# Two-layer decoder trunk on one core: the MLP's second product with one more seven-product tile per pass, its sums gathered by accumulating DMAs

## The chip, the core and the metric

One core of a Trainium2 chip runs the whole kernel in one launch. The metric is device time in microseconds (us), the median of several executions. Before the change it is 2025.09 us (three runs, 2024.75 to 2025.41).

## What is computed

A decoder trunk of two layers over 256 tokens with 2048 channels, in float32. Layer one is a gated short convolution and an MLP, layer two latent attention and an MLP; every half layer ends in a layer norm of the scaled input plus what the half layer gives. The change touches the two MLPs alone:

```python
D_MODEL = 2048; SEQ = 256; D_FF = 4 * D_MODEL; ALPHA = (2 * DEPTH) ** 0.25

def sq_relu_mlp(x, w1, w2):
    return jnp.square(jax.nn.relu(x @ w1)) @ w2

for layer in range(DEPTH):
    mix = short_conv_mixer(...) if layer < N_A else mla_mixer(...)
    h = layer_norm(ALPHA * h + mix, ln_g[layer, 0], ln_b[layer, 0])
    h = layer_norm(ALPHA * h + sq_relu_mlp(h, mlp_w1[layer], mlp_w2[layer]), ln_g[layer, 1], ln_b[layer, 1])
```

## The kernel before

*Precision.* Every float32 operand is split in a high and a low part of type float32r (`split`, L120): ScalarE casts the high part (L122), VectorE subtracts it (L123). A product is three matmuls, high by high, high by low and low by high. `dot` (L282) issues three matmuls of 512 columns. In `mm_run` (L206) the activation is the moving operand with its high and low part side by side: `high` (L200) has 512 columns, `low` (L204) 256.

*Weights.* All weights are one list, `stream`, in the order of use. `take` (L172) hands out the next items and prepares those that follow, until more than `LOOK` = 5 tiles are ahead. A plain item is one transfer of 128 x 1024 (512 KB) from the SP queue into one of five `raw` buffers, split into one of eight pairs of `hi` and `lo` buffers. An item of two transfers (`w2f`) is a tile for seven products: `prepare` (L143 to L166) forms from its four 128 x 512 blocks the combinations that the algorithm wants, with one VectorE operation of 1024 columns (L155) and two of 512 (L158, L161), and splits three tiles of 1024 columns and one of 512 (`t4`). It counts as three tiles.

*The MLP* (`mlp`, L567) goes over the 8192 hidden channels in eight steps q of 1024. A step has two parts. In the first, eight units of W1 (`products`, L273, 32 matmuls each) give 8 x 128 hidden channels into PSUM; `hidden` (L649) brings them out (`whole`, L337: a ScalarE copy and a VectorE add), applies the squared ReLU and splits the result. In the second these 1024 channels are multiplied with W2 and added to `acc` (128 partitions, two halves of 128 tokens, 2048 columns). `acc` has four blocks of 512 columns; `block(n, t)` is block n for the token half t.

*Seven products.* For q = 1 to 6 (`FAST`) the first two blocks go by the Strassen-Winograd scheme: the two token halves, two K tiles of 128 and two blocks make a 2 x 2 by 2 x 2 product, which takes seven products of blocks instead of eight (`FACTORS`, L325). The activation's side wants four combinations, `forms` (made by `form`, L639, in the memory with the tag "a2"). `first_pair` (L603) takes four such tiles, one for each pair of K tiles, and sums the seven products in seven PSUM banks (`KEPT`). `keep` (L595) then adds each bank on VectorE: products 2, 3 and 4 into `acc`, products 1, 5, 7 and 6 (`OWN`) into `sums`. Blocks 2 and 3 follow one after the other by plain products (`down`, L296: four items each, two token halves, two banks), and `put` (L585) adds them to `acc` on VectorE. In the second MLP two small pieces of the residual are turned by TensorE between them (`extra`). In q = 7 `fold` (L612) brings `sums` into `acc` once, six VectorE adds spread over the W1 units; q = 0 and q = 7 have no seven-product tiles.

*Banks.* PSUM has eight banks. The W1 units of q = 1 to 7 use banks 0 and 1 in turn. `first_pair` uses banks 2 to 7 and 0, `down` banks 1 and 2, then 3 and 4.

*Order.* Each engine runs its instructions in the order in which the program has them; the scheduler of the framework fixes that order, also across loops (the preparation of weights is moved ahead of the evacuations that stand before it in the code). TensorE's order is that of the code: per step 256 matmuls of W1, 84 of four seven-product tiles, 96 of eight plain tiles.

## Time and profile before

| | |
|---|---|
| median of three runs | 2025.09 us |
| the profiled execution | 2024.51 us |
| its span, first to last instruction | 2022.5 us |
| TensorE busy | 2015.9 us, 11240 matmuls |
| VectorE busy | 1605.8 us |
| ScalarE busy | 1176.4 us |
| GpSimd busy | 2.3 us, 21 instructions |
| moved by DMA | 385.83 MB, 191 GB/s on average |

A profile line of a group names the source line, the engine, the operation, what is written and read, the shapes and the count; behind the bar stand the busy time, the mean duration in ns, and the idle time of the engine ahead of these instructions with what ended it. PE is TensorE's matmul, PEld its load of weights, DVE VectorE, ACT ScalarE, POOL GpSimd, SP SyncE, which issues the loads. A line of the timeline has the start in us from the start of the span, the duration, and what idle time lay ahead. Matmuls overlap, so the distance of their starts counts, not their duration. A line of the stretches has the window, its length, and for each engine its busy time in it, then TensorE's granted clock, the busy share of the DMA engines, and GB/s.

### The profile page before, as it was taken

What the parts mean: (1) busy time and instruction counts of PE and PEld (TensorE: products, weight loads), DVE (VectorE), ACT (ScalarE), POOL (GpSimd) and SP (SyncE); (2) the same over time, 40 slices, a digit from 0 to 9 for tenths busy, and PEclk for the clock granted to TensorE, in tenths of its full rate; (3) what the DMA queues carried; (4) which work ended last, traced back from release to release, by engine and by line L of the source; (5) the groups of instructions that cost most, each with busy time, mean ns of one, the idle gap of its engine ahead of it and who ended that gap; (6) DMA issues with size and microseconds to landing.
All of it is one profiled execution on the core that took longest, in us unless ns stands there. A gap on an engine that the chain in (4) does not pass through costs nothing.

```text
span 2022.5 us, 30067 instructions
## 1 busy us (share of the span) xinstructions
PE 2015.9 (100%) x11240; PEld 1761.4 (87%) x11240; DVE 1605.8 (79%) x2472; ACT 1176.4 (58%) x1802; POOL 2.3 (0%) x21
## 2 busy tenths in 40 slices
PE   9999999999999999999999999999999999999998
PEld 8888888988888888888889998898888888888886
DVE  8667677788797987979688978776879798797966
ACT  6444445676565665656556655567656556565651
POOL 0000000000000000000000000000000000000000
PEclk9999999999999999999999999999999999999999
DMA  9666666564756647466654544656475664746663
GB/s 322 201 189 188 189 189 192 174 196 144 250 164 202 221 153 249 151 224 209 210 173 152 182 126 137 193 178 194 135 247 176 198 224 140 252 160 205 220 202 119
DMA packets 106849, 385.83 MB, mean 191 GB/s; under 512 B 11856, under 2 KB 12624, under 8 KB 106448
## 3 DMA queue, kind: packets, MB, share of 16 engines
q1 hardware_dynamic: 106560, 383.79, 59.5%
q8 instruction: 88, 1.44, 0.3%
q14 instruction: 57, 0.47, 0.1%
q10 hardware_dynamic: 144, 0.13, 0.0%
HBM read 381.78 MB, written 2.10 MB: 190 GB/s over the span
## 4 chain that ended last, share of the span: by engine, by line
PE 99%; DVE 0%; issue 0%; ACT 0%; DVEq 0%
PE ps_u L200 20%; PE ps_l L200 13%; PE ps_u L204 11%; PE ps_d L284 7%; PE ps_d L286 7%; PE ps_d L285 7%; PE ps_l L204 7%; PE ps_f L285 4%; PE ps_f L286 4%; PE ps_f L284 4%; PE ps_w L234 1%; PE ps_w L232 1%; PE ps_w L233 1%; PE ps_g L234 1%; PE ps_g L232 1%; PE ps_g L233 1%
## 5 line engine op out<-in xcount | busy, mean ns | idle before, releaser
L123 DVE TENSOR_TENSOR lo<-raw,hi 128x1024 fp32r<-128x1024 f32 x710 | 860.0, 1222 | 314.9 <-ACT hi L122 243.2
L122 ACT CAST hi<-raw 128x1024 fp32r<-128x1024 f32 x710 | 742.4, 1050 | 460.5 <-PE ps_u L200 107.9
L200 PE MATMUL ps_u<-xhl,hi 128*128 128x512 f32 x1792 | 621.0, 391 | 0.0
L204 PE MATMUL ps_u<-xhl,lo 128*128 128x256 f32 x1792 | 499.5, 280 | 0.0
L200 PEld LDWEIGHTS ps_u<-xhl,hi 128*128 128x128 f32 x1792 | 334.2, 187 | 72.4
L204 PEld LDWEIGHTS ps_u<-xhl,lo 128*128 128x128 f32 x1792 | 338.6, 189 | 1.8
L284 PE MATMUL ps_d<-hi,h 128*128 128x512 f32 x640 | 249.8, 390 | 0.0
L286 PE MATMUL ps_d<-hi,h 128*128 128x512 f32 x640 | 249.1, 389 | 0.0
L285 PE MATMUL ps_d<-lo,h 128*128 128x512 f32 x640 | 249.0, 389 | 0.0
L200 PE MATMUL ps_l<-xhl_a,hi 128*128 128x512 f32 x704 | 244.1, 393 | 0.0
L204 PE MATMUL ps_l<-xhl_a,lo 128*128 128x256 f32 x704 | 195.4, 279 | 0.0
L200 PEld LDWEIGHTS ps_l<-xhl_a,hi 128*128 128x128 f32 x704 | 132.1, 188 | 29.9
L286 PEld LDWEIGHTS ps_d<-hi,h 128*128 128x128 f32 x640 | 120.1, 188 | 25.0
L284 PEld LDWEIGHTS ps_d<-hi,h 128*128 128x128 f32 x640 | 120.1, 188 | 25.0 <-DVE fh L341 0.3
L285 PEld LDWEIGHTS ps_d<-lo,h 128*128 128x128 f32 x640 | 120.2, 188 | 24.7
L204 PEld LDWEIGHTS ps_l<-xhl_a,lo 128*128 128x128 f32 x704 | 131.9, 188 | 0.2
L654 ACT ACTIVATE fp<-fp 128x256 f32<-128x256 f32 x96 | 40.0, 416 | 73.7 <-DVE fp L341 72.9
L200 PE MATMUL ps_l<-z,hi 128*128 128x512 f32 x240 | 82.4, 391 | 0.0
L122 ACT CAST hi_t<-raw_t 128x1024 fp32r<-128x1024 f32 x48 | 50.4, 1050 | 42.2 <-DVE raw_t L155 33.4
L234 PE MATMUL ps_w<-xd,hi 128*128 128x258 f32 x256 | 72.8, 284 | 0.0
L232 PE MATMUL ps_w<-xd,hi 128*128 128x258 f32 x256 | 72.6, 284 | 0.0
L233 PE MATMUL ps_w<-xd,lo 128*128 128x258 f32 x256 | 72.4, 283 | 0.0
(261 smaller groups left out, 3132.3 us busy)
## 6 DMA issues: line engine op xcount, KB each, us to landing
raw<-in_w_dram SPq DMA_DIRECT2D x416, 512.0 KB, 4.4
raw<-in_w2f_dram SPq DMA_DIRECT2D x96, 512.0 KB, 3.6
raw<-in_w_in_dram SPq DMA_DIRECT2D x88, 512.0 KB, 4.3
raw<-in_w_out_dram SPq DMA_DIRECT2D x32, 512.0 KB, 3.7
raw<-in_w_o_dram SPq DMA_DIRECT2D x32, 512.0 KB, 4.2
raw<-in_w_kv_dram SPq DMA_DIRECT2D x10, 512.0 KB, 3.5
raw<-in_w_q_dram SPq DMA_DIRECT2D x8, 512.0 KB, 4.6
raw<-in_w_uk_dram SPq DMA_DIRECT2D x8, 512.0 KB, 4.6
```

What stands on the lines that cost most here:

```text
L122: nc.scalar.copy(hi, src)
L123: nc.vector.tensor_tensor(lo, src, hi.bitcast(F32), ALU.subtract)
L200: nc.tensor.matmul(ps, w[blk // 8][0][:, blk % 8, :], x, start=first, stop=False)
L204: nc.tensor.matmul(ps[:, :T], w[blk // 8][1][:, blk % 8, :], x[:, :T], start=False, stop=last)
L232: nc.tensor.matmul(ps[:, :W], hi, x[k][:, :W], start=k == 0, stop=False)
L233: nc.tensor.matmul(ps[:, :W], lo, x[k][:, :W], start=False, stop=False)
L234: nc.tensor.matmul(ps[:, :W], hi, x[k][:, W:], start=False, stop=k == NC - 1)
L284: nc.tensor.matmul(ps, x[0], w[0], start=first, stop=False)
L285: nc.tensor.matmul(ps, x[0], w[1], start=False, stop=False)
L286: nc.tensor.matmul(ps, x[1], w[0], start=False, stop=last)
L654: nc.scalar.activation(f, f, AF.Relu)
```

## The change

For q = 1 to 6 the second part has a new order, `down_pairs`, in place of `first_pair` and two calls of `down`:

- Blocks 2 and 3 come first, both at once, in four banks. Their four pairs of K tiles follow `MIXED`: the first by one seven-product tile, the other three by plain products. The plain products add to the banks of products 22, 3, 2 and 4 of that tile ("22" is the product of block 3 with the second token half); the tile's products 1, 5, 7 and 6 are done after it and go into `sums`, which is twice as large. One matmul of each step, the high by low one of product 22 in the last K tile, is issued as two of 256 columns (`EVEN`). `w2f` holds both pairs of blocks.
- Blocks 0 and 1 follow with four seven-product tiles in seven banks. Their sums are copied by ScalarE into `stage` (the memory of `forms`) and added to `acc` and `sums` by DMAs with `accum_op`, issued from the Pool queue. In q = 1 the `OWN` products are copied to `sums` directly.
- The W1 units use four banks in turn; which four, and which the second part uses, moves on by one with each step.
- `fold` has eight adds of 1024 elements per partition. Plain tiles of the second part are taken with a lookahead of 6 instead of 5.

```diff
--- before.py
+++ after.py
@@ -35,6 +35,8 @@
 NB = 4
 BW = D // NB
 FAST = range(1, NQ - 1)
+MIXED = "sppp"
+EVEN = (QC - 1, "22")
 FIRST = (0, 1, 2, 3, 4, 6, 8, 12, 16)
 LEAD = 4
 HEAD = 4
@@ -82,10 +84,13 @@
         out = []
         for q in range(NQ):
             out += halves(w1[l, q * QC:(q + 1) * QC])
-            plain = halves(w2[l, q, 2:] if q in FAST else w2[l, q])
-            fast = [(w2f[l, q, j, 0], w2f[l, q, j, 1]) for j in range(QC // 2)] if q in FAST else []
-            at = 0 if q or q not in FAST else len(plain) // 2
-            out += plain[:at] + fast + plain[at:]
+            if q not in FAST:
+                out += halves(w2[l, q])
+                continue
+            for j, kind in enumerate(MIXED):
+                out += [(w2f[l, q, 1, j, 0], w2f[l, q, 1, j, 1])] if kind == "s" else \
+                    halves(w2[l, q, 3, j]) + halves(w2[l, q, 2, j])
+            out += [(w2f[l, q, 0, j, 0], w2f[l, q, 0, j, 1]) for j in range(QC // 2)]
         return out
 
     stream += mlp_stream(0) + halves(w_kv) + halves(w_q)
@@ -169,14 +174,14 @@
 
         return 1 if len(stream[i]) == 1 else 3
 
-    def take(halves=2):
+    def take(halves=2, look=LOOK):
 
         i = state["next"]
         state["next"] += halves
         ahead = -sum(size(j) for j in range(i, i + halves))
         for j in range(i, len(stream)):
             ahead += size(j)
-            if ahead > LOOK:
+            if ahead > look:
                 break
             if j >= state["split"]:
                 prepare(j)
@@ -279,10 +284,11 @@
             yield ps
 
 
-    def dot(ps, w, x, first, last):
+    def dot(ps, w, x, first, last, two=False):
 
         nc.tensor.matmul(ps, x[0], w[0], start=first, stop=False)
-        nc.tensor.matmul(ps, x[0], w[1], start=False, stop=False)
+        for at in (slice(0, T), slice(T, 2 * T)) if two else (slice(None),):
+            nc.tensor.matmul(ps[:, at], x[0], w[1][:, at], start=False, stop=False)
         nc.tensor.matmul(ps, x[1], w[0], start=False, stop=last)
 
     def held(x, t):
@@ -319,20 +325,20 @@
                     dot(ps, wide_rows(ws[n, k // 2], k % 2), held(x[k], t), k == 0, k == len(x) - 1)
                 put(n, t, ps)
 
-    OWN, KEPT = ("1", "5", "7", "6"), (2, 3, 4, 5, 6, 7, 0)
+    OWN = ("1", "5", "7", "6")
 
 
     FACTORS = (("3", "S4", "22"), ("1", "11", "11"), ("5", "S1", "T1"), ("7", "S3", "T3"),
                ("2", "12", "21"), ("6", "S2", "T2"), ("4", "22", "T4"))
 
-    def fast_products(ps, x, forms, j, n):
+    def fast_products(ps, x, forms, j, fresh, ready):
 
         b, = take(1)
         a = {"11": held(x[2 * j], 0), "12": held(x[2 * j + 1], 0), "22": held(x[2 * j + 1], 1)}
         for i in range(4):
             a[f"S{i + 1}"] = [forms[:, j, o, i * P:(i + 1) * P] for o in range(2)]
         for p, l, r in FACTORS:
-            dot(ps[p], b[r], a[l], j == 0, j == n - 1)
+            dot(ps[p], b[r], a[l], p in fresh, p in ready)
 
     def whole(ps, out):
 
@@ -590,36 +596,70 @@
             else:
                 nc.vector.tensor_tensor(block(n, t), block(n, t), ps, ALU.add)
 
-        sums = fast.tile([P, 4, BW], F32, name=f"sums{idx}")
-
-        def keep(p, ps):
-
-            at = sums[:, OWN.index(p)] if p in OWN else block(*{"2": (0, 0), "3": (1, 0), "4": (0, 1)}[p])
-            if q == 0 or q == FAST[0] and p in OWN:
+        sums = fast.tile([P, 4, 2, BW], F32, name=f"sums{idx}")
+
+        def keep(p, g, ps, staged=None):
+
+            at = sums[:, OWN.index(p), g, :] if p in OWN else \
+                block(*{"2": (2 * g, 0), "3": (2 * g + 1, 0), "4": (2 * g, 1), "22": (2 * g + 1, 1)}[p])
+            if q == FAST[0] and p in OWN:
                 nc.scalar.copy(at, ps)
+            elif staged is not None:
+                nc.scalar.copy(staged, ps)
+                nc.gpsimd.dma_start(at, staged, accum_op=ALU.add)
             else:
                 nc.vector.tensor_tensor(at, at, ps, ALU.add)
 
-        def first_pair(h, forms, banks):
-
+        def down_pairs(h, forms, busy, free):
+
+            ps = {p: psum("ps_d", bank) for p, bank in zip(("22", "3", "2", "4"), free)}
+            fresh = {"22", "3", "2", "4"}
+            for j, kind in enumerate(MIXED):
+                if kind == "s":
+                    first, last = j == MIXED.index("s"), j == MIXED.rindex("s")
+                    if first:
+                        ps.update({p: psum(f"ps_f{p}", bank) for p, bank in zip(OWN, busy)})
+                        fresh.update(OWN)
+                    fast_products(ps, h, forms, j, fresh, OWN if last else ())
+                    fresh &= {"22"}
+                    if last:
+                        for p in OWN:
+                            keep(p, 1, ps[p])
+                    continue
+                if extra and q <= NB and j == len(MIXED) - 1:
+                    for t in range(2):
+                        extra(block, q - 1, t, busy[2 + t])
+                for nb, two in ((3, ((1, "22"), (0, "3"))), (2, ((0, "2"), (1, "4")))):
+                    w, = take(1, LOOK + 1)
+                    for t, p in two:
+                        for kk in range(2):
+                            k = 2 * j + kk
+                            dot(ps[p], wide_rows(w, kk), held(h[k], t), p in fresh, k == QC - 1, (k, p) == EVEN)
+                            fresh.discard(p)
+                    if j == len(MIXED) - 1:
+                        for _, p in two:
+                            keep(p, 1, ps[p])
             n = QC // 2
+            banks = (*busy, *free)
             ps = {p: psum(f"ps_f{p}", bank) for (p, _, _), bank in zip(FACTORS, banks)}
             for j in range(n):
-                fast_products(ps, h, forms, j, n)
-            for p in ps:
-                keep(p, ps[p])
+                fast_products(ps, h, forms, j, ps if j == 0 else (), ps if j == n - 1 else ())
+            stage = act.tile([P, 7, BW], F32, tag="a2", name=f"stage{idx}_{q}")
+            for i, p in enumerate(ps):
+                keep(p, 0, ps[p], stage[:, i, :])
+            return (banks[7], *banks[:3]), banks[3:7]
 
         def fold():
 
             s1, s5, s7, s6 = (sums[:, i] for i in range(4))
-            both = acc[:, 1, :2 * BW].rearrange("p (b c) -> p b c", b=2)
-            right = acc[:, :, BW:2 * BW]
-            two = lambda v: v.unsqueeze(1).to_broadcast([P, 2, BW])
-            for d, a, b in ((block(0, 0), block(0, 0), s1), (s6, s6, s1), (block(1, 0), block(1, 0), s6),
-                            (s7, s7, s6), (both, both, two(s7)), (right, right, two(s5))):
+            c = acc.rearrange("p t (g b c) -> p t b g c", g=2, b=2)
+            for d, a, b in ((c[:, 0, 0], c[:, 0, 0], s1), (s6, s6, s1), (c[:, 0, 1], c[:, 0, 1], s6), (s7, s7, s6),
+                            (c[:, 1, 0], c[:, 1, 0], s7), (c[:, 1, 1], c[:, 1, 1], s7),
+                            (c[:, 0, 1], c[:, 0, 1], s5), (c[:, 1, 1], c[:, 1, 1], s5)):
                 nc.vector.tensor_tensor(d, a, b, ALU.add)
                 yield
 
+        busy, free = (0, 1, 2, 3), (4, 5, 6, 7)
         for q in range(NQ):
             ht = act.tile([P, QC, 2 * T], F32R, tag="c", name=f"h{idx}_{q}")
             h = [ht[:, k, :] for k in range(QC)]
@@ -681,7 +721,7 @@
                 acc = act.tile([P, 2, D], F32, tag="a1", name=f"acc{idx}")
             else:
                 folds = fold()
-                for m, ps in enumerate(products(QC, xhl, TURNED, (0, 1))):
+                for m, ps in enumerate(products(QC, xhl, TURNED, busy)):
                     hidden(m, ps, whole)
                     if q == NQ - 1:
                         next(folds, None)
@@ -695,12 +735,7 @@
                 for n in range(NB):
                     down(h, put, n)
             else:
-                first_pair(h, forms, KEPT)
-                for n, banks in ((2, (1, 2)), (3, (3, 4))):
-                    down(h, put, n, banks)
-                    if extra and n == 2 and q <= NB:
-                        for t in range(2):
-                            extra(block, q - 1, t, 5 + t)
+                busy, free = down_pairs(h, forms, busy, free)
 
     def to_wide(block, put, h):
 
@@ -1093,7 +1128,8 @@
         "w_o": _units(a["mla_w_o"][0]),
         "w1": np.stack([_units(w) for w in a["mlp_w1"]]),
         "w2": np.stack([np.stack([_rows(q) for q in w.reshape(NQ, QC * P, D)]) for w in a["mlp_w2"]]),
-        "w2f": np.stack([np.stack([_pairs(q[:, :2 * BW]) for q in w.reshape(NQ, QC * P, D)]) for w in a["mlp_w2"]]),
+        "w2f": np.stack([np.stack([np.stack([_pairs(q[:, 2 * g * BW:2 * (g + 1) * BW]) for g in range(2)])
+                                   for q in w.reshape(NQ, QC * P, D)]) for w in a["mlp_w2"]]),
         "cosT": np.tile(cos, (4, 1)),
         "sinT": np.tile(np.concatenate([sin, -sin]), (2, 1)),
         "mask": np.concatenate([tri, np.zeros((P, P), np.float32), tri], axis=1),
```

## The prediction

> A *pass* below is one of the twelve turns of the loop over q that the change touches (q = 1 to 6 of each of the two MLPs). Its *W1 part* is eight units of 32 matmuls, its *down part* what the functions `first_pair` and `down` issue. A *seven-product tile* is one item of the weight stream with w2f weights, a *plain tile* one with w2 weights. A time with a + counts from the end of a pass's W1 part.
>
> **What bounds the kernel now.** I read the page first: shares of the engines, then the chain of waits.
>
> ```profile
> span 2022.5 us, 30067 instructions
> PE 2015.9 (100%) x11240; PEld 1761.4 (87%) x11240; DVE 1605.8 (79%) x2472; ACT 1176.4 (58%) x1802; POOL 2.3 (0%) x21
> PE 99%; DVE 0%; issue 0%; ACT 0%; DVEq 0%
> ```
>
> TensorE is busy all of the span and the chain that ended last is 99% TensorE: the time is the number of matmuls times the distance of their starts. That distance is not the mean duration in the groups, since matmuls overlap. The timeline of PE has it; its first column is the start.
>
> ```profile
> 583.26 0.39 PE L284 MATMUL ps_f<-hi,forms 128*128 128x512 f32 x1
> ...
> 602.34 0.39 PE L284 MATMUL ps_d<-hi,h 128*128 128x512 f32 x1
> ...
> 624.10 0.39 PE L200 MATMUL ps_u<-xhl,hi 128*128 128x512 f32 x1
> ```
>
> From 583.26 to 602.34 lie the 84 matmuls of four seven-product tiles, from there to 624.10 the 96 of eight plain tiles: 0.2271 and 0.2267 us each, with no room for a gap. The stretches of this pass, by engine:
>
> ```profile
> core 0: us, PE busy (x) PEld busy (x) DVE busy (x) ACT busy (x) POOL busy (x), PEclk, DMA share, GB/s
> 538.87:583.24 44.37, 44.37 (x257) 39.10 (x256) 34.96 (x52) 27.64 (x45) 0.00 (x0) 1.00 0.50 153
> 583.24:602.32 19.08, 19.08 (x86) 15.79 (x85) 17.62 (x24) 12.10 (x16) 0.00 (x0) 1.00 0.52 157
> 602.32:624.10 21.78, 21.78 (x97) 18.02 (x96) 19.15 (x21) 11.74 (x12) 0.00 (x0) 1.00 0.89 313
> 538.87:624.10 85.23, 85.23 (x437) 72.91 (x436) 71.73 (x96) 51.48 (x72) 0.00 (x0) 1.00 0.60 195
> 965.04:1009.40 44.36, 44.36 (x257) 39.09 (x256) 26.50 (x34) 25.92 (x44) 0.53 (x1) 1.00 0.69 211
> ```
>
> The rows are W1 part, seven-product tiles, plain tiles, the whole pass, and the W1 part of q = 7; the granted clock is 1.00 in each. VectorE is busy 71.73 of 85.23 us (13.5 free), but 17.62 of 19.08 while the seven-product tiles run; the DMA engines are 89% busy only while the plain tiles run. So a matmul that goes is worth its whole 0.227 us, as long as VectorE, ScalarE and the DMAs keep ahead.
>
> **The change, part by part.** *Matmuls.* The first K tile pair of blocks 3 and 4 goes from eight dots of three matmuls to seven: 12 x 3 x 0.2267 = 8.16 us go. `EVEN` splits one 512-wide matmul in two 256-wide. The trace has no such split; the nearest rows are 256-wide matmuls that follow one another:
>
> ```profile
> 1145.04 0.28 PE L218 MATMUL ps_q<-lat,lo 128*128 128x256 f32 x1
> ...
> 1146.95 0.28 PE L219 MATMUL ps_q<-lat,hi 128*128 128x256 f32 x1
> ```
>
> 16 distances in 1.91 us, 0.119 us each. Two cost 0.239 instead of 0.227: 12 x 0.012 = 0.14 us. From both sides: nothing, or two full loads of weights of 0.188 us (first row of the next fence) in place of 0.227, 12 x 0.15 = 1.8 us. I take 0.14, whose rows have the same width and each its own load.
>
> *VectorE and ScalarE.* One seven-product tile takes the place of two plain tiles. The costs are in the groups:
>
> ```profile
> L285 PEld LDWEIGHTS ps_d<-lo,h 128*128 128x128 f32 x640 | 120.2, 188 | 24.7
> L123 DVE TENSOR_TENSOR lo<-raw,hi 128x1024 fp32r<-128x1024 f32 x710 | 860.0, 1222 | 314.9 <-ACT hi L122 243.2 <-issue 46.7 <-PE ps_l L204 21.6
> L155 DVE TENSOR_TENSOR raw_t<-raw,raw 128x1024 f32<-128x1024 f32 x48 | 58.5, 1220 | 5.4 <-DMA raw<-in_w2f_dram 5.2
> L161 DVE TENSOR_TENSOR raw<-raw 128x512 f32<-128x512 f32 x48 | 33.1, 689 | 0.8
> L123 DVE TENSOR_TENSOR t<-raw,t 128x512 fp32r<-128x512 f32 x48 | 32.8, 684 | 0.0
> L601 DVE TENSOR_TENSOR sums<-sums,ps_f 128x512 f32<-128x512 f32 x40 | 26.4, 681 | 0.0
> L122 ACT CAST hi<-raw 128x1024 fp32r<-128x1024 f32 x710 | 742.4, 1050 | 460.5 <-PE ps_u L200 107.9 <-PE ps_d L286 106.3 <-PE ps_l L200 98.0
> L122 ACT CAST t<-raw 128x512 fp32r<-128x512 f32 x48 | 29.6, 616 | 2.1 <-DVE raw L161 2.0
> L599 ACT COPY sums<-ps_f 128x512 f32<-128x512 f32 x8 | 4.5, 586 | 0.2 <-PE ps_f L286 0.2
> ```
>
> VectorE, per pass: one split more (1.222), one `raw_t` (1.220) and three of half size (L158, L161 and the split of `t`, 0.686 each by the two rows shown), 4.50 us more; of eleven adds from PSUM (seven `keep`, four `put`) eight stay, 3 x 0.681 = 2.04 less. Net +2.46 of 13.5 us free: hidden on average. ScalarE, per pass: 1.050 + 0.616 for casts and seven copies of 0.586, +5.8 us on 51.48 of 85.23: hidden. The bytes from HBM stay (a seven-product tile is 1 MB, two plain tiles are 1 MB). `fold` has eight adds of 1024 elements instead of four of 512 and two of 1024: 6 x 1.222 - 4 x 0.681 = 4.6 us more in q = 7, where VectorE is busy 26.50 of 44.36 us: hidden.
>
> *Order.* Six plain tiles now stand between the first seven-product tile and the other four, and these four end the pass. Until the last dot of the last one (4.76 + 6 x 2.72 + 3 x 4.76 + 6 x 0.68 = +39.4 us) VectorE has: the rest of the last W1 unit (an evacuation, two half splits, four forms of 0.28, 2.9), eight adds from PSUM (5.4), about three of the six plain splits (3.7; the eight weight buffers let the others run in the W1 part), four seven-product tiles of 3 x 1.222 + 1.220 + 3 x 0.686 = 6.94 each (27.8): 39.8 us. But its operations overlap when nothing makes them wait:
>
> ```profile
> 559.39 1.22 DVE L155 TENSOR_TENSOR raw_t<-raw,raw 128x1024 f32<-128x1024 f32 x1 [0.51 <-DMA raw<-in_w2f_dram]
> 560.53 1.22 DVE L123 TENSOR_TENSOR lo<-raw,hi 128x1024 fp32r<-128x1024 f32 x1
> 561.67 0.28 DVE L644 TENSOR_TENSOR sf<-fp 128x128 f32<-128x128 f32 x1
> ```
>
> 1.14 us apart for a duration of 1.22; over 46 operations that is 3.7 us less, 36.1 against 39.4. I take it as hidden, since four such tiles keep VectorE 92% busy today (17.62 of 19.08) without a wait on TensorE. At 92% and no overlap it would be 39.8 / 0.92 = 43.3, 3.9 us late in each pass. Both ends stay for the range.
>
> *Banks.* The sixth dot of the first tile writes the PSUM bank of the last W1 unit, at +3.40 us (15 x 0.2267). The evacuation of that unit, in a pass whose W1 part ends at 1711.38:
>
> ```profile
> 1711.38 0.39 PE L284 MATMUL ps_f<-hi,forms 128*128 128x512 f32 x1
> ...
> 1714.42 0.42 DVE L341 TENSOR_TENSOR fp<-ps_u,t 128x256 f32<-128x256 f32 x1
> ```
>
> It ends at +3.46, a wait of 0.06 us. Before, that bank was first wanted after the 84 matmuls of the seven-product tiles. I take 0.1 us in all; if one more cast and split came ahead (1.05 + 1.22) it would be 2.3 us in each pass. With four W1 banks instead of two an evacuation may come three units late instead of one; no W1 part is longer than its 256 matmuls today, so nothing is gained.
>
> *Accumulating DMAs.* The last seven sums are copied by ScalarE into `stage` and added by 76 DMAs of 256 KB from the Pool queue, where 21 small instructions stand today. `stage` has the memory of `forms`: the copies wait for the last use of `forms`, the sixth dot of the last tile, and the next pass writes `forms` only after all seven DMAs have landed. In the program of the changed kernel that wait stands in ScalarE's order behind the evacuation of the second W1 unit, as here:
>
> ```profile
> 641.80 0.36 ACT L340 COPY t<-ps_u 128x256 f32<-128x256 f32 x1
> 642.08 0.62 ACT L122 CAST forms<-sf 128x512 fp32r<-128x512 f32 x1
> ```
>
> 642.08 - 624.10 = 18.0 us after the W1 part begins. No accumulating DMA is in the trace. Nearest rows, issue to landing:
>
> ```profile
> raw<-in_w_dram SPq DMA_DIRECT2D x416, 512.0 KB, 4.4
> out_dram<-acc SPq DMA_DIRECT2D x8, 256.0 KB, 2.4
> xres<-in_xT_dram SPq DMA_DIRECT2D x2, 256.0 KB, 6.9
> ```
>
> `out<-acc` moves 256 KB of the same tile: seven one after another take 16.8 us and land before 18.0. From both sides: all at once after the last copy, or 6.9 us each, 48 us. I take 2.4, as size and tile agree: no wait. The Trainium skill ("DMA: Bandwidth & Descriptors", section "Anatomy of one DMA — SWDGE (gpsimd) path") gives about 2.0 us plus bytes over 436 GB/s; an estimate from it is 2.6 us each, 18.2 in a row, and the sum would stay as it is, since ScalarE would wait 0.2 us. No run here shows it yet.
>
> *Sum.* -8.16 + 0.14 + 0.1 = -7.9 us. The profiled execution took 2024.51 us (span 2022.5 and 2.0 around it), 0.6 below the median 2025.09; so 2016.6 for such an execution, and 2017.2 as a median.
>
> **Rivals.**
>
> *The accumulations come late* (slower). ScalarE and VectorE both stand at `forms` from 18.0 us on, with the casts and splits of later weights behind them. TensorE has weights and banks until about 31 us (the seventh unit wants the third's bank at 6 x 5.55 = 33.3, and its evacuation stands behind `forms`), but VectorE's arrears must be made up before the next down part: in the W1 part it has 44.37 - 34.96 = 9.4 us free. So TensorE loses once seven DMAs take over 18.0 + 9.4 = 27.4 us, 3.9 each in a row. At the 4.4 us of a 512 KB load (an accumulation reads its target too), 30.8 us: 3.4 us lost in ten passes (q = 1 has three such DMAs), 2017 + 34 = 2051 us. For it: the DMA engines are 50% busy in the W1 part already. Against it: 2.4 us for the same size, and seven from one queue need not run one by one. The Trainium skill ("SBUF — State Buffer", section "A bandwidth-pool intuition that's wrong") has a DMA of this queue that takes 0.62 us alone take 3.1 beside a VectorE copy that holds the shared port; by it, an estimate, 7 x (2.4 + 2.5) = 34 us and 2017 + 69 us. Its rule names copies; VectorE's rows in a pass are all TENSOR_TENSOR, which that page exempts.
>
> *VectorE becomes the bound at the end of the pass* (slower). The 3.9 us above in each pass are +47; half of it, 2 us, gives 2017 + 24 = 2041. For it: 92% busy among seven-product tiles, and no plain tiles behind them to catch up. Against: the fourth such tile now starts 16 us later, with six plain tiles ahead of it.
>
> *The bank of the last unit* (gain spent). 0.5 us in each pass: 2017 + 6 = 2023; at 2.3, 2045. Against it: the end of that evacuation at +3.46.
>
> *The distances in the W1 part depend on what ran before* (no gain, or a loss). A pair of one 512- and one 256-wide matmul takes 44.37 / 128 = 0.347 us. At two weight loads of 0.188 in a row it would be 0.376: 12 x 128 x 0.029 = 45 us, 2062; at a fifth of that, 2026. Against it: a pass keeps an even number of matmuls, and 512-wide ones still precede the W1 part.
>
> **How the numbers follow.** The forecast has 0.64; its own range is 2015.5 to 2019.5 (0.2 us per pass). Late accumulations 0.13, VectorE at the end 0.11, the bank 0.07, the distances 0.05. A measurement tells 0.2%, about 4 us, from no change: faster means below 2021.0, slower above 2029.1. Faster: the forecast and small waits at the bank, 0.67; same, from the bank, the distances and a little of VectorE, 0.08; slower 0.25. The range reaches down to 2015 and up to 2041 (VectorE 2 us late): 0.64 + 0.07 of the bank, 0.07 of VectorE, 0.04 of late DMAs is 0.82.
>
> **What would show it.** Right: 24 matmuls fewer; passes of 85.23 - 0.66 = 84.57 us; no gap over 0.3 us in the down part; a group of 76 copies into `stage`; a new DMA queue, its landings less than 18 us behind the end of the pass. Late accumulations: `forms` on ACT or DVE waits for a DMA, and PE has gaps late in the W1 part. VectorE late: gaps in the last three seven-product tiles, and no idle time of VectorE there. Bank: a gap 15 matmuls into the down part. Distances: W1 parts longer than 44.37 us without a gap. The forecast fails if seven accumulations take over 27 us, or if four seven-product tiles cost VectorE more than they do today.

## The result and the profile after

The changed kernel takes 2243.4 us (median of four runs, 2241.6 to 2245.4); the kernel before took 2024.9 us beside it. The ratio is 1.108, with an interval of 1.1066 to 1.1093: slower by 218 us, and outside the forecast's range (2015 to 2041).

The page of the changed kernel: the span, the busy times, the granted clock in 40 slices, the shares of the chain that ended last, and the two groups of the new DMAs among the issues (count, size, median us to landing).

```profile
span 2241.5 us, 30289 instructions
PE 2071.1 (92%) x11216; PEld 1792.0 (80%) x11216; DVE 1646.5 (73%) x2500; ACT 1223.5 (55%) x1910; POOL 68.9 (3%) x97
PEclk9999999999998989998999999999999898999899
PE 53%; issue 36%; DVE 4%; DMA 3%; POOL 2%; ACT 2%; POOLq 0%; DVEq 0%; ACTq 0%
sums<-stage POOLq DMA_DIRECT2D x40, 256.0 KB, 3.3
acc<-stage POOLq DMA_DIRECT2D x36, 256.0 KB, 4.0
```

From the groups of the same kernel, the copies into `stage`:

```profile
L608 ACT COPY stage<-ps_f 128x512 f32<-128x512 f32 x76 | 39.7, 608 | 0.0
```

There are 11216 matmuls, 24 fewer, as forecast (36 go, the split adds 12). But TensorE has only 53% of the chain where it had 99%, and the granted clock, 1.00 in the stretches before, is below 0.9 in six of the 40 slices, all of them in the passes. The 76 copies and the 76 DMAs are there.

The waits of the changed kernel (engine, line, for what: us in total, times, longest):

```profile
ACT forms L127 <- DMA acc<-stage: 161.6, 9, 20.8
DVE forms L128 <- ACT forms L127: 158.8, 10, 20.1
PE ps_f L289 <- DVE fp L347: 82.6, 27, 5.3
PE ps_u L205 <- DVE fp L347: 63.0, 8, 9.1
DVE acc L659 <- DMA acc<-stage: 33.8, 2, 17.1
```

`forms` on ScalarE waits for a DMA, and VectorE waits for ScalarE there; TensorE then waits for evacuations (`fp`), in the W1 part (`ps_u`) and more often in the down part (`ps_f`). The last row is the `fold` of q = 7, which waits up to 17.1 us for the last DMAs. The stretches of one pass (q = 3 of the first MLP): W1 part, down part, the whole pass, and a stretch from the down part.

```profile
632.86:686.81 53.95, 46.45 (x257) 40.49 (x256) 26.86 (x37) 26.39 (x43) 6.13 (x7) 0.94 0.63 186
686.81:741.76 54.95, 45.12 (x181) 35.87 (x179) 47.77 (x61) 29.08 (x40) 0.00 (x0) 0.84 0.50 156
632.86:741.76 108.90, 91.57 (x436) 76.36 (x434) 74.64 (x97) 55.48 (x82) 6.13 (x7) 0.89 0.57 171
690.29:708.00 17.71, 9.21 (x22) 6.50 (x21) 14.69 (x24) 11.31 (x18) 0.00 (x0) 0.52 0.50 148
```

Before, these were 44.37, 40.86 and 85.23 us (the pass in the prediction). The W1 part is 9.6 us longer, the down part 14.1, and in the 17.71 us of the last row, which begin 3.5 us into the down part, the granted clock is 0.52. The same pass by POOL's timeline, then ScalarE's and TensorE's:

```profile
634.62 0.89 POOL L609 DMA_DIRECT2D acc<-stage  x1 [76.64 <-ACT stage L608]
642.49 0.87 POOL L609 DMA_DIRECT2D sums<-stage  x1 [6.99 <-issue]
...
656.54 0.87 POOL L609 DMA_DIRECT2D sums<-stage  x1 [5.17 <-issue]
...
667.21 0.88 POOL L609 DMA_DIRECT2D acc<-stage  x1 [2.69 <-issue]
...
670.62 0.62 ACT L127 CAST forms<-sf 128x512 fp32r<-128x512 f32 x1 [19.00 <-DMA acc<-stage]
...
666.05 0.28 PE L209 MATMUL ps_u<-xhl,lo 128*128 128x256 f32 x1
673.83 0.79 PE L205 MATMUL ps_u<-xhl,hi 128*128 128x512 f32 x1 [7.50 <-DVE fp L347]
...
690.29 0.39 PE L292 MATMUL ps_f<-hi_t,forms 128*128 128x512 f32 x1
695.97 0.76 PE L289 MATMUL ps_f<-hi_t,forms 128*128 128x512 f32 x1 [5.30 <-DVE fp L347]
696.53 0.63 PE L291 MATMUL ps_f<-lo_t,forms 128*128 128x512 f32 x1
696.96 0.63 PE L292 MATMUL ps_f<-hi_t,forms 128*128 128x512 f32 x1
```

The seven DMAs start 7.9, 8.0, 6.1, 3.6, 3.5 and 3.6 us apart (650.48, 660.14 and 663.65 are not shown). From issue to landing they take 7.6, 7.7 and 5.8 us, and then 3.2 to 3.3; each starts 0.3 us after the one before has landed, and POOL's idle time between them ends with "issue", no event that the profile shows. The DMA engines are 99 to 100% busy during the first three, and 45 to 49% during the last four: the last weight load of this stretch is issued at 652.39 and lands at 657.52. ScalarE stands 19 us until the last has landed; the cast of `forms` comes at 670.62, 37.8 us into the W1 part. Behind it the evacuation of the third unit is late, so the seventh unit has no bank: TensorE's gap at 666.05. In the down part three products wait in turn for the banks of the last three units: TensorE is idle 1.33 us at 689.71, 5.30 at 695.97 and 3.20 at 702.07. A gap is given below as the distance of the starts of two matmuls. After the gap of 5.7 us (690.29 to 695.97) the matmuls start 0.43 us apart instead of 0.227 (696.53 to 696.96; ahead of them 0.56): a gap also costs clock. In the passes of both MLPs there are 37 gaps over 0.7 us, 179 us together, 171 of them beyond the usual 0.227 each; 2243.4 - 2017.2 = 226 us are lost against the forecast, so some 55 us are such slow matmuls and small waits. The Trainium skill ("TensorE: Matmul & The Clock Gate", "Part 1: The HAM clock gate") has the clock halve after about 3.4 us without work and return after as much work. The 0.43 us of a 512-column matmul, not quite twice 0.227, agree, though shorter gaps were at times enough here (last section).

### The profile page after: what moved, and what is told of

The parts are those of the page before. It is cut to its first block, busy times and chain, and to the rows that moved or that the text cites. A ratio compares the mean times of both kernels' runs of the same rounds, so it can differ in the third digit from the quotient of the medians.

```text
span 2241.5 us, 30289 instructions
## 1 busy us (share of the span) xinstructions
PE 2071.1 (92%) x11216; PEld 1792.0 (80%) x11216; DVE 1646.5 (73%) x2500; ACT 1223.5 (55%) x1910; POOL 68.9 (3%) x97
## 3 DMA queue, kind: packets, MB, share of 16 engines
q0 software_dynamic: 10944, 19.93, 5.0%
## 4 chain that ended last, share of the span: by engine, by line
PE 53%; issue 36%; DVE 4%; DMA 3%; POOL 2%; ACT 2%; POOLq 0%; DVEq 0%; ACTq 0%
PE ps_l L205 12%; PE ps_l L209 6%; PE ps_u L205 5%; PE ps_d L289 4%; PE ps_d L292 4%; PE ps_d L291 4%; PE ps_u L209 3%; DVE lo L128 2%; POOL sums L609 1%; PE ps_w L239 1%; PE ps_w L237 1%; PE ps_w L238 1%; DMA raw<-in_w_dram 1%; ACT hi L127 1%; POOL acc L609 1%
## 5 line engine op out<-in xcount | busy, mean ns | idle before, releaser
L205 PE MATMUL ps_u<-xhl,hi 128*128 128x512 f32 x1792 | 644.6, 402 | 63.0 <-DVE fp L347 63.0
L205 PEld LDWEIGHTS ps_u<-xhl,hi 128*128 128x128 f32 x1792 | 345.5, 193 | 142.4 <-DVE fp L347 65.5
L289 PE MATMUL ps_d<-hi,h 128*128 128x512 f32 x556 | 223.0, 401 | 2.0 <-DVE fh L347 2.0
L291 PE MATMUL ps_d<-lo,h 128*128 128x512 f32 (+1 forms) x568 | 221.0, 393 | 0.0
L292 PE MATMUL ps_d<-hi,h 128*128 128x512 f32 x556 | 220.7, 397 | 0.0
L128 DVE TENSOR_TENSOR forms<-sf,forms 128x512 fp32r<-128x512 f32 x48 | 32.9, 685 | 159.0 <-ACT forms L127 158.8
L127 ACT CAST forms<-sf 128x512 fp32r<-128x512 f32 x48 | 29.8, 621 | 196.5 <-DMA acc<-stage 161.6
L289 PEld LDWEIGHTS ps_d<-hi,h 128*128 128x128 f32 x556 | 108.3, 195 | 25.1 <-DVE fh L347 2.4
L292 PEld LDWEIGHTS ps_d<-hi,h 128*128 128x128 f32 x556 | 107.1, 193 | 22.8
L127 ACT CAST hi_t<-raw_t 128x1024 fp32r<-128x1024 f32 x60 | 63.1, 1051 | 93.8 <-DVE raw_t L160 80.1
L289 PE MATMUL ps_f<-hi_t,forms 128*128 128x512 f32 x120 | 50.4, 420 | 48.1 <-DVE fp L347 48.1
L160 DVE TENSOR_TENSOR raw_t<-raw,raw 128x1024 f32<-128x1024 f32 x60 | 73.1, 1219 | 25.5 <-DMA raw<-in_w2f_dram 25.5
```

Of the source, the lines that this page charges most:

```text
L127: nc.scalar.copy(hi, src)
L128: nc.vector.tensor_tensor(lo, src, hi.bitcast(F32), ALU.subtract)
L160: nc.vector.tensor_tensor(t.rearrange(two, a=2), b12.unsqueeze(1).to_broadcast([P, 2, BW]), r1.rearrange(two, a=2), ALU.subtract)
L205: nc.tensor.matmul(ps, w[blk // 8][0][:, blk % 8, :], x, start=first, stop=False)
L289: nc.tensor.matmul(ps, x[0], w[0], start=first, stop=False)
L291: nc.tensor.matmul(ps[:, at], x[0], w[1][:, at], start=False, stop=False)
```

## The experiments

Each kernel below is the changed kernel with the edit that is shown or told; `...` in a diff stands for the rest of a line. "+" times count from the start of a W1 part here, unless the down part is named.

**1. VectorE adds.** Sums straight from PSUM, no copies, no DMAs.

```diff
-            stage = act.tile([P, 7, BW], F32, tag="a2", ...)
-            for i, p in enumerate(ps):
-                keep(p, 0, ps[p], stage[:, i, :])
+            for p in ps:
+                keep(p, 0, ps[p])
```

> The seven sums of the first two blocks are added by VectorE straight from PSUM; no copies into stage, no accumulating DMAs. Theory A (two losses: the casts of forms wait for seven accumulating DMAs that run one after another, and, apart from them, the banks of the last two W1 units are evacuated late): the 8 to 9 us gaps late in each W1 part and the 17 us wait of fold go; what stays is what q = 2 shows, where no DMA had been waited for: gaps of 1.9 and 5.0 us early in the down part, so 2017 + 12 x (2 to 7) = 2041 to 2101 us. Theory B (the DMAs are only where a late VectorE shows; it has too much to do at the end of each pass): VectorE gets seven adds more, 4.8 us per pass, so no better than 2243 us. Theory C (the distances in W1 changed): W1 parts without a gap stay longer than 44.4 us.

2027.9 us, ratio to before 1.0015 (1.0006 to 1.0025), better than theory A's range. So 215 of the 226 us hang on the copies and DMAs, and not on VectorE, which has 4.8 us more work per pass. Every W1 part is 44.39 us: the distances did not change. What stays is one gap in 11 of 12 passes, 0.7 to 2.0 us, 11.7 us in all (9.2 beyond the usual distance), at the sixth product of the first tile:

```profile
672.89 0.39 PE L292 MATMUL ps_d<-hi,h 128*128 128x512 f32 x1
674.87 0.50 PE L289 MATMUL ps_f<-hi,forms 128*128 128x512 f32 x1 [1.59 <-DVE fp L347]
...
669.21 0.28 DVE L683 TENSOR_TENSOR sf<-fp 128x128 f32<-128x128 f32 x1
672.12 1.22 DVE L160 TENSOR_TENSOR raw_t<-raw,raw 128x1024 f32<-128x1024 f32 x1 [2.63 <-DMA raw<-in_w2f_dram]
674.40 0.42 DVE L347 TENSOR_TENSOR fp<-ps_u,t 128x256 f32<-128x256 f32 x1
```

TensorE (first two rows) wants the bank of the last W1 unit at 673.1, +3.4 us into the down part as forecast. VectorE evacuates it at 674.40 only: ahead of it in its order stands `raw_t` of a later seven-product tile, which waits 2.63 us for its weights, and one more split.

**2. The copies without the DMAs** (this kernel leaves out the later terms of these sums).

```diff
                 nc.scalar.copy(staged, ps)
-                nc.gpsimd.dma_start(at, staged, accum_op=ALU.add)
```

> The copies into stage stay and the accumulating DMAs are left out (so the sums of the first two blocks lack their later terms): the price of the DMAs alone, without VectorE's adds. Theory A: the waits at forms vanish, the late banks in the down part stay: 2035 to 2100 us, at or below the kernel with VectorE adds. Theory B: VectorE has 4.8 us per pass less than with its own adds, so clearly below that kernel by up to 12 x 4.8 = 58 us. A third theory (ScalarE's copies, waiting for the last use of forms, hold up the evacuations of the next W1 part): 2150 us or more.

2034.9 us (ratio 1.0041 to 1.0074): 7 us above the kernel with VectorE adds, though VectorE has seven adds less. The DMAs themselves cost 2243.4 - 2034.9 = 208 us.

**3. Three larger DMAs** (1 MB into `sums`, 512 and 256 KB into `acc`, over the same bytes).

> The seven DMAs of 256 KB become three, of 1 MB, 512 KB and 256 KB, over the same bytes. If each DMA has a fixed price that is paid in a row (theory A1, one at a time with some 2 us fixed): three of them land by some 20 us, no wait at forms, the time of the kernel without DMAs, below 2110 us. If the price goes by bytes or packets in contention with the weight loads (A2): the last lands as late as before, some 37 us, and the time stays at 2200 to 2245 us.

2153.3 us, between the two. Under weight loads the 512 KB took 6.5 us from its issue to the next and the 1 MB 12.2, where 256 KB had taken 7.9: the price goes neither by the bytes alone nor by the number of DMAs alone. (The Pool queue has 4896 packets here for the same bytes, and 10944 in the changed kernel; what they cost was not taken apart.) The first cast of `forms` came at +28.5 to +30 us, the gaps late in the W1 part went, and the down parts stayed at 53.7 to 55.2 us.

**4 and 5. More descriptor memory,** with its control (one `t4` buffer instead of two makes the room).

```diff
-... name=f"t4_{i}", bufs=2)
+... name=f"t4_{i}", bufs=1)
-dynamic_dma_scratch_size=512
+dynamic_dma_scratch_size=4096      # the second kernel only
```

> Control for the next kernel: the changed kernel with one T4 buffer instead of two, which frees 4 KB per partition; descriptor memory as it is (512 bytes per partition). All theories: as the changed kernel, 2225 to 2265 us; if the second T4 buffer carries something, more.

> As the control, with 4096 bytes per partition of descriptor memory for the Pool queue's DMAs instead of 512. Theory A1 (the memory holds the descriptors of one DMA, so the next one is written only when the one before has landed): POOL's idle time between the DMAs of one pass goes, all seven are on their way within 10 us of the first, they share the DMA engines and the seventh lands by 15 to 25 us after the start of the W1 part: 2040 to 2150 us. Theory A2 (they share the engines with the weight loads and each takes its 7 to 8 us whatever stands in the queue; or the queue itself goes one by one): seventh landing near 37 us and a time within 1% of the control.

2256.5 us for the control, 2129.6 us with 4096 bytes: 127 us less. The first and the last of POOL's rows and ScalarE's cast in the timeline of that kernel, and, from the view of `stage`, us from issue to landing (min, median, max):

```profile
633.50 0.86 POOL L609 DMA_DIRECT2D acc<-stage  x1 [87.91 <-ACT stage L608]
...
637.58 2.27 POOL L609 DMA_DIRECT2D acc<-stage  x1
...
656.74 0.62 ACT L127 CAST forms<-sf 128x512 fp32r<-128x512 f32 x1 [2.69 <-DMA acc<-stage]
```

```profile
DMA to landing us min/median/max: 6.2/11.4/19.2
```

All seven are issued within 5 us, with at most 0.17 us of idle time between them, so the one-by-one turn came from the 512 bytes. They still land only by 656.7, +25.8 us: beside the others and the weight loads a DMA takes 11.4 us (median). ScalarE waits 2.7 us at `forms` and not 19, since it comes there only at +23.1; and yet some 95 us more than without DMAs (2129.6 against 2034.9) are lost, most of it at banks in the down parts, 49.9 to 51.6 us long.

**6. The first tile second** (VectorE adds, `MIXED = "pspp"`).

> VectorE adds (no DMAs), and the seven-product tile of the last two blocks comes second, behind the two plain tiles of the first K tile pair (pspp for sppp). Theory A (the 11.7 us of gaps in the kernel with VectorE adds are the banks of the last W1 units, wanted 3.40 us into the down part and free at 4 to 5): now they are wanted 5.4 us later, the gaps go, 24 matmuls' worth of 8.16 us stay: 2016 to 2018.5 us. Rival (VectorE is late in general: the wait moves to the next place, the tiles at the end of the pass): 2022 to 2030 us.

2038.8 us (ratio 1.0059 to 1.0084), above both ranges. The bank gaps went, and new ones came in the first and the last of the four tiles at the end of the pass, which now wait for their own preparation: the place that the rival named. A line of TensorE in one of them, and its wait for the split of `t4`:

```profile
868.03 0.47 PE L289 MATMUL ps_f<-t,h 128*128 128x512 f32 x1 [1.46 <-ACT t L127]
```

That the tile, placed first, has the W1 part as cover for its preparation, and so leaves VectorE the time for the last tiles, is a reading; no run tests it.

**7. Plain writes instead of accumulation** (this kernel leaves out all but the last terms of the sums).

```diff
-nc.gpsimd.dma_start(at, staged, accum_op=ALU.add)
+nc.gpsimd.dma_start(at, staged)
```

> The 76 DMAs write instead of accumulating (so the sums keep only their last terms); queue, count, bytes and order stay. If the accumulation itself is dear (reading the target, adding): each lands in clearly less than 7.9 us under the weight loads and 3.5 us without them, and the time falls well below 2200 us. If the queue's turn (descriptors written by POOL, one DMA at a time) sets the price: 2200 to 2245 us, the same 6 to 8 us from one issue to the next.

2069.5 us. By the time the first of the two holds, by the landings it does not: a write takes 5.7 to 6.2 us from issue to landing (medians), where the accumulations took 3.3 to 4.0, but more than one is on its way at a time; POOL issued the seven over 11.7 us, and the first cast came at +19 to +21 us. The Pool queue took 2.4% of the DMA engines' time for its 19.93 MB, and 5.0% with accumulation. A plain write has 80 packets where an accumulation has 144. How much of the gain is the overlap and how much the missing accumulation was not taken apart.

**8 and 9. The bank last, and no split.** With VectorE adds, the order of the products in the first tile becomes 3, 1, 5, 2, 7, 4, 6; the second kernel also drops `EVEN`.

> VectorE adds (no DMAs); in the seven-product tile of the last two blocks the product in the bank of the last W1 unit comes last of the seven and the one in the bank before it fifth (3, 1, 5, 2, 7, 4, 6), so the last bank is wanted 4.08 us into the down part instead of 3.40. Theory A (the 11.7 us of gaps in the kernel with VectorE adds are that bank, free at 3.3 to 5.1 us): 0.68 us less in each of 12 passes where 0.7 us or more were lost, so 2018 to 2021 us. Rival (the wait moves on, since VectorE is late in general): 2024 to 2030 us.

> As the kernel before it in this call, without EVEN: no matmul split in two, so each pass has an odd number of matmuls. If the parity carries something (the matmuls of the W1 parts alternate 512 and 256 columns): some W1 parts are longer than 44.39 us, up to 45 us in all. If not: 0.1 us less, no difference that can be measured.

2023.3 us (ratio 0.9986 to 1.0004) and 2022.1 (0.9978 to 0.9995); the first lies between the two ranges. Of the eleven gaps over 0.7 us four and three are left. Without the split every W1 part stays at 44.39 us: the split and the even count carry nothing.

**10 and 11. Two and four DMAs** (products 3 and 2; products 3, 1, 5 and 7), the other sums by VectorE.

> The changed kernel with two of the seven sums (products 3 and 2) by accumulating DMAs, five by VectorE. Theory A (only a landing behind the first cast of forms, 18 us into the next W1 part, costs anything; at 7.9 us each under weight loads the second lands at 17.5 us): first cast at 18 to 20 us, no stand, down parts of 41 to 44 us, 2025 to 2045 us. Rival (any accumulating DMA slows the weight loads enough to hurt): 2060 us or more.

> Four of the seven sums by accumulating DMAs (products 3, 1, 5 and 7), three by VectorE. Theory A: the fourth lands 26 to 28 us into the W1 part; the kernel with three larger DMAs had its first cast at 28.5 to 30 us and down parts of 53.7 to 55 us instead of 41. Eight passes and the fold are struck: 2028 + 8 x 12.5 = 2110 to 2150 us. By the prediction's own reckoning (no loss below 27.4 us): 2030 to 2045 us.

2044.5 and 2127.4 us. With two, the first cast behind them stands at +17.2 to +19.4 us and the down parts are 41.3 to 43.4 us (+20.8 and 45.1 once); the 17 us above experiment 1 come with no wait of `forms` for a DMA, and were not taken apart. With four, the cast comes at +25.6 to +27.9 in the eight passes behind four DMAs, and their down parts are 51.1 to 53.8: the loss begins below the prediction's 27.4 us.

**12. The spare bank.** VectorE adds, no split; the sum that only plain tiles write takes the last W1 unit's bank, and product 6 the bank that this sum had. The changed parts of the lines:

```diff
-zip(("22", "3", "2", "4"), free)
+zip(("22", "3", "2", "4"), (busy[3], *free[1:]))
-zip(OWN, busy)
+zip(OWN, (*busy[:3], free[0]))
-extra(block, q - 1, t, busy[2 + t])
+extra(block, q - 1, t, (busy[2], free[0])[t])
-((3, ((1, "22"), (0, "3")))
+((3, ((0, "3"), (1, "22")))
```

> VectorE adds, no EVEN, products in their old order; in the down part the sum that only plain tiles write (22) takes the bank of the last W1 unit, and product 6 takes the bank that 22 had. The last W1 unit's bank is then wanted 6.1 us into the down part instead of 3.40. Theory A (what is left above 2017 is that bank): no gap over 0.4 us at the sixth product, 2016 to 2019 us, and the kernel beats the one before by 0.3 to 0.4%. Rival (the wait moves on to the next tiles, as it did in the kernel with the tile second): 2021 to 2028 us.

2018.5 us, ratio 0.9971 (0.9960 to 0.9982): faster than the kernel before by 0.3%. The stretches of its pass q = 3 (W1 part, down part, pass), and from its timeline two rows of VectorE at the start of that down part:

```profile
623.11:667.50 44.39, 44.39 (x257) 39.12 (x256) 39.63 (x56) 31.39 (x48) 0.00 (x0) 1.00 0.74 251
667.50:707.66 40.16, 40.16 (x179) 33.24 (x178) 37.78 (x48) 20.19 (x27) 0.00 (x0) 1.00 0.40 134
623.11:707.66 84.55, 84.55 (x434) 72.36 (x433) 77.41 (x103) 51.58 (x74) 0.00 (x0) 1.00 0.58 195
```

```profile
670.33 1.22 DVE L160 TENSOR_TENSOR raw_t<-raw,raw 128x1024 f32<-128x1024 f32 x1 [2.21 <-DMA raw<-in_w2f_dram]
672.61 0.42 DVE L347 TENSOR_TENSOR fp<-ps_u,t 128x256 f32<-128x256 f32 x1
```

The last unit is still evacuated late (672.61, behind the same `raw_t`), and nothing waits for it. VectorE is busy 77.41 of 84.55 us, and TensorE has no gap.

**13. The wait without DMAs.** VectorE adds; POOL writes zeros over the memory of `forms` seven times behind each pass.

> VectorE adds, no accumulating DMAs, but the memory of forms is kept busy behind each pass by seven writes of zeros from POOL (3584 elements per partition each; by the 0.53 us of one of 512 elements an estimate of 3.7 us each, 26 us in all), so the first cast of forms waits until some 24 us into the W1 part, with no DMA traffic. Theory A (the lateness alone costs): down parts of 49 to 52 us as where the DMAs land at 24 to 26 us, 2028 + 8 to 10 passes x 9 = 2100 to 2130 us. Rival (the cost is the DMA traffic, which delays weight loads, and arrears at forms are made up in the W1 part): 2025 to 2045 us.

2026.2 us (ratio 0.9996 to 1.0017), in the rival's range. The writes took 3.10 us each, not the estimated 3.7, and the first cast came at +21.7 to +22.6 us. The ten down parts behind it are 40.2 to 41.9 us, but for one of 44.3: a cast that late costs little. But the scheduler had also put that cast further back in ScalarE's and VectorE's order (18 operations behind the first evacuation of the pass instead of 14 or 15), and ScalarE stood only 0.3 us for it in all, so this run does not settle what a longer stand costs.

**14 and 15. The traffic without the wait,** with its control (VectorE adds, one `t4` buffer): seven accumulating DMAs per pass into a buffer that nothing reads.

> VectorE adds and, beside them, seven accumulating DMAs of 256 KB per pass from acc into a buffer that nothing reads (one T4 buffer instead of two makes room for it; no DMAs in the last seven-product pass of a layer): the traffic without anyone waiting for it. Theory A: no stand at forms; weight loads are slower while they run; within 20 us of the kernel without them beside it in this call. Rival (the traffic is what costs): 2090 us or more.

> Control for the kernel before it: VectorE adds, one T4 buffer, no DMAs. 2028 to 2045 us (with seven DMAs the second T4 buffer was worth 13 us).

2069.1 us (two runs, 2061.9 and 2076.4) against 2031.9 (2029.5 to 2032.9): the traffic alone costs about 37 us, more than theory A allowed and less than the rival. Of the waits, the one for the weights of a seven-product tile grew, in total and in its longest; the traffic kernel's row is first, the control's second:

```profile
DVE raw_t L160 <- DMA raw<-in_w2f_dram: 48.9, 31, 4.3
```

```profile
DVE raw_t L160 <- DMA raw<-in_w2f_dram: 35.2, 30, 2.4
```

Here VectorE works on while the DMAs run. Two stretches of this kernel, each from the issue of one of its DMAs to the next:

```profile
656.75:660.66 3.91, 3.91 (x25) 3.46 (x24) 3.91 (x7) 3.04 (x6) 0.88 (x2) 1.00 0.64 173
660.66:669.18 8.52, 8.52 (x51) 7.50 (x50) 7.03 (x12) 6.47 (x12) 0.86 (x1) 1.00 0.88 266
```

In the first VectorE is busy all of the time, few weight loads are on their way (the DMA engines are 64% busy), and the DMA lands within 3.5 us. In the second five weight loads are on their way (88%), and the DMA takes 8.1 us. So the weight loads make these DMAs slow, and not the work of VectorE beside them, as the rival of a shared port would have it.

**16. The wait without the traffic.** VectorE adds; seven DMAs in each pass add zeros of 16 columns, 8 KB each, from the memory of `forms` to the seven targets. The scheduler's order on VectorE around the casts is that of experiment 1.

> VectorE adds as before; beside them, in each pass, seven accumulating DMAs add zeros of 16 columns (8 KB instead of 256 KB) from the memory of forms to the same seven targets, so that the casts of forms wait for seven DMAs one by one, with a thirty-second of the bytes. Theory A (the wait alone costs once it is long): if the seven land 25 us or more into the W1 part, first casts there and down parts of 49 us or more, 2100 us or more; if the time of such a DMA goes by its bytes, they land by 18 us and the time is 2025 to 2035 us, which leaves the question to the place of the first cast. Rival (only the traffic costs): 2025 to 2045 us wherever the first cast stands.

2137.5 us, 110 us above experiment 1. From its timeline POOL's rows, ScalarE's cast and a gap of TensorE in the next down part; from its page the Pool queue (packets, MB, share):

```profile
637.33 0.88 POOL L610 DMA_DIRECT2D acc<-stage  x1 [0.41 <-POOL stage L647]
643.41 0.87 POOL L610 DMA_DIRECT2D sums<-stage  x1 [5.21 <-DVE acc L608]
...
662.71 0.88 POOL L610 DMA_DIRECT2D acc<-stage  x1 [1.44 <-issue]
...
664.88 0.62 ACT L127 CAST forms<-sf 128x512 fp32r<-128x512 f32 x1 [9.90 <-DMA acc<-stage]
...
687.46 0.47 PE L289 MATMUL ps_f<-hi_t,forms 128*128 128x512 f32 x1 [3.64 <-DVE fp L347]
```

```profile
q0 software_dynamic: 12096, 0.69, 1.0%
```

With 0.69 MB in all instead of 19.93 the DMAs still stand 4 to 6 us apart under weight loads (6.1, 4.6, 5.2, 4.1), 2.3 without them, and the first casts come at +26.7 to +30.6. The down parts are 49.3 to 53.6 us. The waits for weights are nearly what they were (`raw_t` 25.6 us in all, 26.1 in experiment 1; `hi` of the plain tiles 79.7 and 73.2), so the late cast loses the time, and not the traffic. The Trainium skill ("DMA: Bandwidth & Descriptors", "Queues, rings and completion order") has a DMA engine go round between queues by whole packets. That a small DMA waits its turn among large ones fits that and these distances; no run here tests it.

All in one view, for the pass q = 3 of the first MLP (start of the first cast of `forms` behind the start of the W1 part; length of the down part that follows, from the timelines):

| kernel | first cast | down part |
|---|---|---|
| two DMAs (10) | +17.52 | 42.14 |
| before | +17.98 | 40.84 |
| plain writes (7) | +18.97 | 44.76 |
| VectorE adds (1) | +19.14 | 42.09 |
| spare bank (12) | +20.26 | 40.16 |
| traffic alone (14) | +20.54 | 48.16 |
| zeros by POOL (13) | +22.57 | 44.32 |
| four DMAs (11) | +25.76 | 51.15 |
| large descriptor memory (5) | +25.81 | 50.79 |
| small DMAs (16) | +27.70 | 51.41 |
| three DMAs (3) | +29.19 | 55.22 |
| changed kernel | +37.76 | 54.95, and 9.6 in the W1 part |

Two rows lie off the order, plain writes and traffic alone: large DMAs run there, and the down part is long though the cast is not late. The row of zeros by POOL is the one long pass of ten.

## Why the prediction was wrong

*What held.* The matmuls that go are worth their 0.227 us: in the kernel with the spare bank the pass is 84.55 us, forecast 84.57. The split costs nothing that shows. VectorE's load hides: in that kernel, with seven more adds a pass than forecast, no gap stands in the last tiles. The W1 distances do not change.

*What failed first: the price of an accumulating DMA,* 2.4 us taken from the `out<-acc` row. That row is a plain write by another queue, 20 us and more after the last weight load had landed. Measured from issue to landing: 7.6 us under weight loads, 3.3 without, one at a time, 36.0 us for the seven (634.62 to 670.62). The 2.6 us that the prediction estimated beside it are short too. The upper bound, 48 us in all, had the 36; the value taken did not. By the prediction's own reckoning a landing at +37.8 would have cost 37.8 - 27.4 = 10.4 us in ten passes, about 2120 us. The rest of the way to 2243 is the next point.

*What failed second: the point from which lateness counts.* The rival "late accumulations" named the place (`forms`, then the seventh unit's bank, then the down part), but set the point at 18.0 + 9.4 = 27.4 us, because VectorE has 9.4 us free in a W1 part. Most of that time lies ahead of the stand. The same stretch of the kernel before, cut at its first cast of `forms` (VectorE is the third of the busy times):

```profile
538.87:556.85 17.98, 17.98 (x105) 15.83 (x104) 10.64 (x16) 9.96 (x16) 0.00 (x0) 1.00 0.61 185
556.85:583.24 26.39, 26.39 (x154) 23.27 (x153) 24.32 (x37) 17.68 (x31) 0.00 (x0) 1.00 0.42 131
```

VectorE has 7.3 us free ahead of the cast and 26.39 - 24.32 = 2.1 behind it, so the same reckoning from the right rows gives 18.0 + 2.1, about 20 us. Nor does a late VectorE work without a pause. In the changed kernel, after the stand (VectorE, then ScalarE):

```profile
671.27 0.69 DVE L128 TENSOR_TENSOR forms<-sf,forms 128x512 fp32r<-128x512 f32 x1 [18.31 <-ACT forms L127]
675.19 1.23 DVE L128 TENSOR_TENSOR lo<-raw,hi 128x1024 fp32r<-128x1024 f32 x1 [1.42 <-ACT hi L127]
...
673.81 0.42 ACT L694 ACTIVATE fp<-fp 128x256 f32<-128x256 f32 x1 [1.35 <-DVE fp L347]
679.26 0.42 ACT L694 ACTIVATE fp<-fp 128x256 f32<-128x256 f32 x1 [2.57 <-DVE fp L347]
684.85 0.62 ACT L127 CAST forms<-sf 128x512 fp32r<-128x512 f32 x1 [0.92 <-DVE sf L686]
693.79 0.62 ACT L127 CAST forms<-sf 128x512 fp32r<-128x512 f32 x1 [0.56 <-DVE sf L686]
```

The two engines wait for each other in turn, up to 2.57 us at a time. From the first to the third cast of `forms` (670.62, 684.85, 693.79) they need 23.2 us, with VectorE busy for 18.1 of them; in the kernel before the casts stood at 17.98, 31.20 and 42.28 us, 24.3 us. They make up 1.1 us in two pairs of units, not 9.4 in four. (That the waits in turn keep them from more is read from these rows; no run varies them.) What is not made up arrives at the banks of the last W1 units. By the table and the pass of experiment 12 with the latest cast (+21.6, a down part of 40.8) hardly anything is lost to the cast up to there. The passes q = 2 of the changed kernel, behind three DMAs only, have casts at +25.2 and +24.2 and lose 8.6 and 5.9 us in the down part; from +25.8 on it is 10 us of each pass and more. Small DMAs with a first cast at +27.7 should have cost 0.3 us by the prediction, and cost 10.6 (51.41 - 40.84).

*The bank of the last unit* was taken at 0.1 us in all, with 2.3 us a pass as the bound. With VectorE adds it shows as gaps of 0.7 to 2.0 us in 11 passes. The row used (+3.46) came from the old order; in the new one a wait for weights stands ahead of that evacuation, in the changed kernel too (`raw_t` waits 2.16 us at 699.32, the evacuation comes at 701.60). The bound had this case, the choice did not.

*What was left out:* the granted clock. 171 us of gaps became 226 us of time, in the main since matmuls behind a long gap start 0.43 us apart. And the copies: 7 us more than VectorE's adds, though ScalarE has the time on average. Why was not tried.

Of the 208 us that the DMAs cost, the wait alone is worth about 110 (experiment 16 against 1, at first casts of +27 to +31 in ten passes; the changed kernel has eight passes behind seven DMAs and two behind three) and the traffic alone about 37 (14 against 15). The rest goes with the longer stand at +38 and with both together, and was not taken apart.

## What to carry to other kernels

Free time of an engine can make up for a stall only where it lies behind the stall: cut the stretch there before you count (2.1 us of 9.4 here). Where its operations wait in turn for another engine, look at how far apart the same step recurs, not at the sum of idle time. Price an operation that the trace lacks by a row under the load that it will meet: here a transfer's time rose from 3.3 to 7.6 us by the weight loads beside it. Before a bank is reused early in a stage, see what stands ahead of its evacuation in the evacuating engine's order in the new program; a bank that is wanted later anyway can make the wait vanish (0.5%, 2027.9 to 2018.5 us).

## What the runs showed of the hardware

- With 512 bytes per partition of descriptor memory an accumulating DMA of 256 KB from the Pool queue goes alone: the next starts 7.9 us later under weight loads, 3.5 us later without. With 4096 bytes seven are issued in 5 us.
- A DMA of 8 KB in the same place costs far more than its share of the bytes: 4 to 6 us from one to the next under weight loads, 2.3 without (7.9 and 3.5 for 256 KB).
- Accumulating takes the DMA engines about twice the time of plain writing: 5.0% of a span of 2241.5 us against 2.4% of one of 2068.6 us, for the same 19.93 MB (with 144 packets each against 80).
- After a gap of TensorE of 5.7 us its 512-column matmuls start 0.43 us apart instead of 0.227. In the passes of all these kernels no gap up to 2.1 us did that. Between 2.2 and 3.4 us some did and some did not: 2.20 us (experiment 14) was followed by seven matmuls at 0.43, 2.85 (experiment 10) and 3.39 (experiment 11) by none.
